# Three 256-column products per k-tile in the MLP up-projections, summed in half a PSUM bank

## The chip, the cores and the metric

The kernel runs on one core of a Trainium2 chip, in one launch. The metric is the device time of one execution in microseconds (us); shorter is better. The profile is of one execution, recorded on the same core, and its times are microseconds from the first instruction unless they are marked ns. PE is TensorE's stream of matrix products and PEld its stream of weight loads, DVE is VectorE, ACT is ScalarE, POOL is GpSimd and SP is SyncE.

## The reference, cut to what matters

The model is a trunk of two layers on 256 tokens of width 2048. Layer 0 has a bidirectional state-space mixer with a gated output, layer 1 has windowed attention. After each of the two stands the same kind of MLP, and only its first half is touched here:

```python
def rms_norm(x, gain):
    y = xf * lax.rsqrt(jnp.mean(xf * xf, axis=-1, keepdims=True) + NORM_EPS)
    return y * gain

def sqrelu_mlp(h, w_up, w_down):          # w_up 2048 x 8192, w_down 8192 x 2048
    return jnp.square(jax.nn.relu(h @ w_up)) @ w_down

h = h + sqrelu_mlp(rms_norm(h, mlp_norm[i]), mlp_w_up[i], mlp_w_down[i])
```

All inputs and the output are float32.

## The kernel before, in words

Products of float32 operands are made from a high and a low part. A weight block arrives by DMA (`wload`, L655 to L669), ACT rounds it to the high part `hi` (L667), and DVE subtracts to get the low part `lo` (L668). Activations are split in the same way when they are written (`norm_post`, L716, for the MLP's input). A product `x @ w` is then the sum of three: high by high, low by high, and high by low. `wnext` (L679) hands out the next split block and keeps one more in preparation; there are two buffers for raw blocks, three for high parts and three for low parts, used in turn.

`mlp` (L813) has two parts. The **up-projection** walks over 64 blocks of 128 hidden units (`fb`). For each block it takes one weight block of 16 k-tiles (128 x 128 each) and one PSUM bank of 512 float32 columns. The tokens are the moving operand. The activations lie in `act`, as 16 k-tiles, each with its high part (256 tokens) next to its low part (256 tokens). `up_mm` (L825) issues two products for each k-tile: L827 multiplies the high weights with both parts at once, 512 columns wide, so that the left half of the bank collects high by high and the right half high weights by low activations; L828 multiplies the low weights with the high activations, 256 columns wide, into the left half. So a bank ends with two halves that have to be added.

`up_post` (L830) does that: ACT copies the right half to SBUF (L832), DVE adds the left half to the copy (L834), DVE applies the rectifier and the tokens' norm factor `rb` (L835), and ACT squares into `hT` (L836). The order of issue is: products of block `fb`, then `up_post` of block `fb - 1`. The first two blocks are special: their first 12 k-tiles are issued before the last part of the layer's input is normalised (`fin`, the steps of the stage ahead), and their last 4 after it.

The **down-projection** (`down`, L874) has 64 k-tiles of 128 hidden units; for each it issues 24 products of 512 columns (L878), from the three combinations, four column blocks and two token halves, into eight banks.

Every product is issued with its own load of the stationary operand. Each engine works its queue in order. The MLP runs twice, after the state-space layer and after the attention layer.

Of the kernel before, what the change touches and what calls it, by code (L numbers as in the profile page):

```python
# [9 lines left out]
F32 = mybir.dt.float32  # L10
# [3 lines left out]
ALU = mybir.AluOpType  # L14
AX = mybir.AxisListType

P = 128
D = 2048
L = 256
# [73 lines left out]
class Ring:  # L93
# [3 lines left out]
    def next(self):  # L97
        self.i = (self.i + 1) % len(self.tiles)
        return self.tiles[self.i]
# [63 lines left out]
def drain(g):  # L163
    for _ in g:
        pass


class Kernel:
# [644 lines left out]
    def mlp(self, nxt, fin):  # L813
        nc, ar = self.nc, self.ar
        pe = nc.tensor
        last = nxt is None
        pool = Scope(ar, "ml", 2, 48128)
        rb = pool.tile([P, L], F32, name="rb", bufs=1)
        hTs = [ar.get("hT#%d" % i, [n, L], at=o) for i, (n, o) in enumerate(((32, 31744), (16, 39936), (16, 44032)))]

        def hT(kt):
            return hTs[0][:, kt] if kt < 32 else hTs[kt // 16 - 1][:, kt % 16]
        act = self.act

        def up_mm(bk, wh, wl, kts):  # L825
            for kt in kts:
                pe.matmul(bk, lhsT=wh[:, kt], rhs=act[:, kt].rearrange("p x c -> p (x c)"), start=(kt == 0), stop=False)  # L827
                pe.matmul(bk[:, :L], lhsT=wl[:, kt], rhs=act[:, kt, 0], start=False, stop=(kt == KT - 1))  # L828

        def up_post(fb, bk):  # L830
            t = pool.tile([P, L], F32, name="up_t")
            nc.scalar.copy(t, bk[:, L:])  # L832
            s = pool.tile([P, L], F32, name="up_s")
            nc.vector.tensor_add(s, bk[:, :L], t)  # L834
            nc.vector.scalar_tensor_tensor(s, s, 0.0, rb, op0=ALU.max, op1=ALU.mult)  # L835
            nc.scalar.activation(hT(fb), s, AF.Square)  # L836

        def wup():
            return (w.rearrange("p (k c) -> p k c", k=KT) for w in self.wnext())
        early = []  # L840
        next(fin)
        next(fin)
        for fb in range(2):
            wh, wl = wup()
            bk = self.bank()
            up_mm(bk, wh, wl, range(12))
            early.append((bk, wh, wl))
            next(fin)
        drain(fin)
        for tt in range(2):  # L850
            self.norm_end(tt)
        for fb in range(2):
            up_mm(*early[fb], range(12, KT))
        self.rstd_row(rb)
        for fb in range(2):
            up_post(fb, early[fb][0])
        post = None
        for fb in range(2, FF // P):
            wh, wl = wup()
            bk = self.bank()  # L860
            up_mm(bk, wh, wl, range(KT))
            if post:
                up_post(*post)
            post = (fb, bk)
        NK = FF // P

        def split(kt):
            hh = pool.tile([P, L], F32R, name="hh", bufs=3)
            hl = pool.tile([P, L], F32R, name="hl", bufs=3)
            nc.scalar.copy(hh, hT(kt))  # L870
            nc.vector.tensor_sub(hl, hT(kt), hh.bitcast(F32))  # L871
            return hh, hl

        def down(kt, tt, hh, hl, wh, wl, cbs=range(4)):  # L874
            ts = slice(tt * P, (tt + 1) * P)
            for x, w in ((hh, wh), (hl, wh), (hh, wl)):
                for cb in cbs:
                    pe.matmul(bks[tt][cb], lhsT=x[:, ts], rhs=w[:, cb * 512:(cb + 1) * 512],  # L878
                              start=(kt == 0 and w is wh and x is hh), stop=(kt == NK - 1 and w is wl))
        nx = split(0)  # L880
        w0 = self.wnext()
        up_post(*post)
        ar.free("act")
        bks = [[self.bank() for _ in range(4)] for _ in range(2)]
        pend = []
        for kt in range(NK):
            hh, hl = nx
            wh, wl = self.wnext() if kt else w0
            if kt + 1 < NK:
                nx = split(kt + 1)  # L890
            if kt == NK // 2 + 4 and not last:
                ar.free("hT#0")
                hx = ar.get("hx", [2, 4, 512], at=31744)
                gains = ar.get("hg", [D], at=35840)
                nc.sync.dma_start(gains, self.d["gains"][nxt])
            if kt < NK - 2:
                for tt in range(2):
                    down(kt, tt, hh, hl, wh, wl)
            else:
                pend.append((kt, hh, hl, wh, wl))  # L900
        ar.free("hT")
        if not last:
            self.norm_begin(nxt)

        def end(tt, cb):
            cs = slice(cb * 512, (cb + 1) * 512)
            gain = None if last else gains[:, cs]
            nc.vector.tensor_add(self.resid[:, tt, cs], self.resid[:, tt, cs], bks[tt][cb])
            if last:
                nc.sync.dma_start(self.d["out"][:, tt, cs], self.resid[:, tt, cs])  # L910
            else:
                self.norm_pre(cb, tt, gain, hx[:, tt, cb])
                if cb == 3:
                    self.norm_end(tt)

        def post(tt):
            for cb in range(4):
                self.norm_post(cb, tt, hx[:, tt, cb])
                yield
        for tt in range(2):  # L920
            n = 0 if last else len(pend) - 1
            for p in pend[:n]:
                down(p[0], tt, *p[1:])
            for cb in range(4):
                for p in pend[n:]:
                    down(p[0], tt, *p[1:], cbs=(cb,))
                end(tt, cb)
        pool.close()
        if not last:
            drain(post(0))  # L930
            return post(1)
# [466 lines left out]
```

## Time and profile before

| what | value |
|---|---|
| time, median of 3 runs | 2107.94 us (2106.41 to 2108.83) |
| profiled execution, first to last instruction | 2103.6 us |
| PE busy | 2030.6 us, 13,844 products |
| PEld busy | 1705.0 us, 13,844 loads |
| DVE busy | 1245.0 us |
| ACT busy | 974.7 us |
| up-projection of the first MLP | 386 to 757 us |
| up-projection of the second MLP | 1394 to 1751 us |

The profiled execution has no device time of its own beside its span; the three timed runs lie 2.8 to 5.2 us above that span, for what happens ahead of the first and behind the last instruction. In a table of stretches, each engine's busy time in the stretch is followed by the number of instructions in brackets, and PEclk is the clock granted to TensorE as a share of full speed. In a list of groups, the columns are line, engine, operation, output and inputs, shapes and count, then busy time and the mean of one in ns, then the idle time just before them and what ended it. A product's own duration contains the time it takes to run through the array, which overlaps with the product behind it; the time that one costs in a dense stream is the distance from its start to the next start.

### The profile page before, as it was taken

The page shows a single profiled execution, that of the slowest core. Times are in us where ns is not written, and L with a number is a line of the kernel's source. Part 1 is how long each engine was busy: PE and PEld are TensorE (multiplying, and loading weights), DVE is VectorE, ACT ScalarE, POOL GpSimd, SP SyncE. Part 2 cuts the span into 40 slices and gives each one's busy share as a digit, 9 for nine tenths or more (in the row PEclk, how much of TensorE's full clock was granted, in tenths as well). Part 3 has the DMA queues.
Part 4 walks back from the last instruction along what each step waited for, and adds up shares of the span by engine and source line. Part 5 has one row for each costly group of instructions (what it writes and reads, how often), then busy time and mean ns, then how long its engine had stood idle before and what let it go on. Part 6 is the DMA issues. An engine that isn't in the chain of part 4 may idle for free.

```text
span 2103.6 us, 33054 instructions
## 1 busy us (share of the span) xinstructions
PE 2030.6 (97%) x13844; PEld 1705.0 (81%) x13844; DVE 1245.0 (59%) x1824; ACT 974.7 (46%) x1238; POOL 331.0 (16%) x248
## 2 busy tenths in 40 slices
PE   4989999999999999999999889999999999999999
PEld 4877778788888888888887667888888888888887
DVE  8889736655555554444556877465555555444444
ACT  6553645444444444434434556554444444443442
POOL 6988721200000000000003330100000000000000
PEclk9999999999999999999999999999999999999999
DMA  3224455455555555655554332455555555555554
GB/s 120 73 93 144 152 199 196 154 200 188 193 180 184 193 184 200 213 188 199 202 186 153 115 128 96 146 185 200 188 193 186 195 184 196 200 187 193 200 187 153
DMA packets 59685, 364.28 MB, mean 173 GB/s; under 512 B 6816, under 2 KB 9152, under 8 KB 19600
## 3 DMA queue, kind: packets, MB, share of 16 engines
q1 hardware_dynamic: 54144, 342.32, 46.4%
q10 hardware_dynamic: 5184, 19.49, 2.8%
q8 instruction: 108, 1.77, 0.3%
q0 software_dynamic: 208, 0.36, 0.0%
q14 instruction: 41, 0.34, 0.0%
HBM read 360.05 MB, written 2.10 MB: 172 GB/s over the span
## 4 chain that ended last, share of the span: by engine, by line
PE 75%; DVE 4%; ACT 2%; DMA 1%; issue 1%; POOL 0%; SPq 0%; ACTq 0%; DVEq 0%
PE bank L878 33%; PE bank L827 23%; PE bank L828 11%; PE bank L686 2%; PE bank L687 2%; PE bank L688 2%; DVE slot L668 1%; ACT slot L667 1%; ACT slot L1039 1%; PE bank L1058 1%; DMA slot<-in_wqkv 1%; PE bank L1049 1%; DVE slot L1043 1%; DVE slot L1024 1%; DMA slot<-in_wup 0%
## 5 line engine op out<-in xcount | busy, mean ns | idle before, releaser
L668 DVE TENSOR_TENSOR slot<-slot,slot 128x2048 fp32r<-128x2048 f32 (+1 forms) x321 | 713.6, 2225 | 737.0 <-ACT slot L667 733.3
L667 ACT CAST slot<-slot 128x2048 fp32r<-128x2048 f32 (+2 forms) x357 | 623.5, 1752 | 743.0 <-PE bank L878 368.4
L827 PE MATMUL bank<-slot,slot 128*128 128x512 f32 x2048 | 720.0, 397 | 0.0
L878 PE MATMUL bank<-slot,slot 128*128 128x512 f32 x3072 | 696.7, 389 | 0.0
L878 PEld LDWEIGHTS bank<-slot,slot 128*128 128x128 f32 x3072 | 576.5, 188 | 119.6
L828 PE MATMUL bank<-slot,slot 128*128 128x256 f32 x2048 | 572.0, 280 | 0.0
L827 PEld LDWEIGHTS bank<-slot,slot 128*128 128x128 f32 x2048 | 385.5, 188 | 92.5
L828 PEld LDWEIGHTS bank<-slot,slot 128*128 128x128 f32 x2048 | 386.9, 189 | 0.3
L686 PE MATMUL bank<-slot,slot 128*128 128x512 f32 x544 | 217.3, 401 | 6.8 <-ACT slot L667 5.2
L688 PE MATMUL bank<-slot,slot 128*128 128x512 f32 x544 | 207.7, 395 | 8.3 <-POOL slot L668 8.1
L687 PE MATMUL bank<-slot,slot 128*128 128x512 f32 x544 | 213.6, 393 | 0.0
L686 PEld LDWEIGHTS bank<-slot,slot 128*128 128x128 f32 x544 | 102.7, 189 | 31.4 <-ACT slot L667 6.5
L836 ACT ACTIVATE slot<-slot 128x256 f32<-128x256 f32 x128 | 53.6, 420 | 160.4 <-DVE slot L835 160.4
L688 PEld LDWEIGHTS bank<-slot,slot 128*128 128x128 f32 x544 | 101.6, 188 | 32.0 <-POOL slot L668 10.1
L687 PEld LDWEIGHTS bank<-slot,slot 128*128 128x128 f32 x544 | 102.8, 189 | 20.4 <-issue 0.5
L668 POOL TENSOR_TENSOR slot<-slot,slot 128x1024 fp32r<-128x1024 f32 (+2 forms) x36 | 101.1, 2818 | 102.5 <-ACT slot L667 97.2
L949 POOL DMA_DIRECT2D slot<-in_pos x1 | 0.8, 754 | 613.1 <-DVE slot L871 613.1
L532 DVE TENSOR_TENSOR bank<-bank,slot 128x256 f32<-128x256 f32 x126 | 54.4, 431 | 4.1
L835 DVE SCALAR_TENSOR_TENSOR slot<-slot 128x256 f32<-128x256 f32 x128 | 54.2, 425 | 4.2
L704 POOL TENSOR_TENSOR slot<-slot 128x512 f32<-128x512 f32 x16 | 28.9, 1814 | 170.6 <-DVE slot L1157 61.5
L870 ACT CAST slot<-slot 128x256 fp32r<-128x256 f32 x128 | 51.0, 400 | 8.3 <-PE bank L878 8.3
L871 DVE TENSOR_TENSOR slot<-slot,slot 128x256 fp32r<-128x256 f32 x128 | 53.3, 419 | 1.7 <-ACT slot L870 1.6
(217 smaller groups left out, 1389.0 us busy)
## 6 DMA issues: line engine op xcount, KB each, us to landing
slot<-in_wup SPq DMA_DIRECT2D x128, 1024.0 KB, 4.8
slot<-in_wdn SPq DMA_DIRECT2D x128, 1024.0 KB, 4.8
slot<-in_wqkv SPq DMA_DIRECT2D x20, 1024.0 KB, 4.9
slot<-in_wge ACTq DMA_DIRECT2D x32, 512.0 KB, 3.7
slot<-in_wgl SPq DMA_DIRECT2D x16, 1024.0 KB, 5.3
slot<-in_wo SPq DMA_DIRECT2D x16, 1024.0 KB, 4.9
slot<-in_bz SPq DMA_DIRECT2D x16, 336.0 KB, 3.5
slot<-in_cp SPq DMA_DIRECT2D x16, 256.0 KB, 2.7
```

Of the source, the lines that this page charges most:

```text
L532: yield v.tensor_mul(xy, lb, st[:, k - 1].rearrange("p r (o g) -> p r o g", o=1).broadcast_to([P, 2, 2, n]))
L667: self.nc.scalar.copy(hi[:, c], raw[:, c])
L668: (self.nc.gpsimd if e == "g" else self.nc.vector).tensor_sub(lo[:, c], raw[:, c], hi[:, c].bitcast(F32))
L686: pe.matmul(out, lhsT=xh, rhs=wh, start=first, stop=False)
L687: pe.matmul(out, lhsT=xl, rhs=wh, start=False, stop=False)
L688: pe.matmul(out, lhsT=xh, rhs=wl, start=False, stop=last)
L827: pe.matmul(bk, lhsT=wh[:, kt], rhs=act[:, kt].rearrange("p x c -> p (x c)"), start=(kt == 0), stop=False)
L828: pe.matmul(bk[:, :L], lhsT=wl[:, kt], rhs=act[:, kt, 0], start=False, stop=(kt == KT - 1))
L835: nc.vector.scalar_tensor_tensor(s, s, 0.0, rb, op0=ALU.max, op1=ALU.mult)
L836: nc.scalar.activation(hT(fb), s, AF.Square)
L871: nc.vector.tensor_sub(hl, hT(kt), hh.bitcast(F32))
L878: pe.matmul(bks[tt][cb], lhsT=x[:, ts], rhs=w[:, cb * 512:(cb + 1) * 512], start=(kt == 0 and w is wh and x is hh), stop=(kt == NK - 1 and ...
```

## The change

`up_mm` issues three products of 256 columns for each k-tile instead of one of 512 and one of 256: high weights by high activations, high weights by low activations, and low weights by high activations. All three add into the left half of the bank, and the right half stays unused. Within a block all 32 products with high weights come first and then the 16 with low weights; before, the two kinds alternated. In `up_post` the copy and the add are gone, and the rectifier reads the left half of the bank directly. The same `up_mm` and `up_post` serve both MLPs and their first two, divided blocks.

```diff
         def up_mm(bk, wh, wl, kts):
             for kt in kts:
-                pe.matmul(bk, lhsT=wh[:, kt], rhs=act[:, kt].rearrange("p x c -> p (x c)"), start=(kt == 0), stop=False)
+                for x in range(2):
+                    pe.matmul(bk[:, :L], lhsT=wh[:, kt], rhs=act[:, kt, x], start=(kt == 0 and x == 0), stop=False)
+            for kt in kts:
                 pe.matmul(bk[:, :L], lhsT=wl[:, kt], rhs=act[:, kt, 0], start=False, stop=(kt == KT - 1))
 
         def up_post(fb, bk):
-            t = pool.tile([P, L], F32, name="up_t")
-            nc.scalar.copy(t, bk[:, L:])
             s = pool.tile([P, L], F32, name="up_s")
-            nc.vector.tensor_add(s, bk[:, :L], t)
-            nc.vector.scalar_tensor_tensor(s, s, 0.0, rb, op0=ALU.max, op1=ALU.mult)
+            nc.vector.scalar_tensor_tensor(s, bk[:, :L], 0.0, rb, op0=ALU.max, op1=ALU.mult)
             nc.scalar.activation(hT(fb), s, AF.Square)
```

## The prediction

> **What bounds the kernel now.** I read the page's head first, then its chain of waits, then tables by stretch for the two stages that the change touches.
>
> ```profile
> span 2103.6 us, 33054 instructions
> PE 2030.6 (97%) x13844; PEld 1705.0 (81%) x13844; DVE 1245.0 (59%) x1824; ACT 974.7 (46%) x1238; POOL 331.0 (16%) x248
> ...
> PE 75%; DVE 4%; ACT 2%; DMA 1%; issue 1%; POOL 0%; SPq 0%; ACTq 0%; DVEq 0%
> PE bank L878 33%; PE bank L827 23%; PE bank L828 11%; PE bank L686 2%; PE bank L687 2%; PE bank L688 2%; DVE slot L668 1%; ACT slot L667 1%; ACT slot L1039 1%; PE bank L1058 1%; DMA slot<-in_wqkv 1%; PE bank L1049 1%; DVE slot L1043 1%; DVE slot L1024 1%; DMA slot<-in_wup 0%
> ```
>
> PE carries the chain. The up-projections' two lines hold 34% of it; no line of `up_post` appears. An average over the span doesn't say that the stage itself is bound by PE, so next come the two up-projections whole, from the first L827 to the first L878:
>
> ```profile
> 386.00:756.60 370.60, 366.17 (x2063) 0.99 0.52 182
> 1394.20:1751.30 357.10, 357.10 (x2064) 1.00 0.54 189
> ```
>
> The second column is PE's busy time. In the second MLP PE never stops; in the first it stands idle for 4.43 us, in one piece ahead of a transpose:
>
> ```profile
> 390.32 0.28 PE L828 MATMUL bank<-slot,slot 128*128 128x256 f32 x1
> 395.04 0.47 PE L713 MATMUL bank<-ident,slot 128*128 128x128 f32 x1 [4.43 <-POOL slot L704]
> ```
>
> That wait is for the input's norm (L704, the gain multiply of the stage ahead), which the change leaves alone. So in both stages the time is what PE's products cost, start to start. Here is that cost, in dense stretches of the first up-projection, the first down-projection, the second up- and the second down-projection (columns: stretch, PE busy with its products, clock, DMA):
>
> ```profile
> 440.00:740.00 300.00, 300.00 (x1700) 1.00 0.53 187
> 760.00:1090.00 330.00, 330.00 (x1458) 1.00 0.56 198
> 1420.00:1740.00 320.00, 320.00 (x1847) 1.00 0.55 191
> 1760.00:2080.00 320.00, 320.00 (x1414) 1.00 0.55 194
> ```
>
> Down-projections hold only 512-column products: 330/1458 = 226.3 ns each, and 320/1414 = 226.3 in the second layer. An up-projection's k-tile is two products: 300/850 = 352.9 ns in the first layer, 320/923.5 = 346.5 in the second, for 768 columns. All four at clock 1.00.
>
> How much of that is columns? One short stretch ran at half clock; below its row in the table of stretches are two rows of the timeline:
>
> ```profile
> 396.60:400.40 3.80, 3.80 (x13) 0.50 0.00 0
> ```
>
> ```profile
> 396.59 0.63 PE L827 MATMUL bank<-slot,slot 128*128 128x512 f32 x1
> ...
> 400.43 0.63 PE L827 MATMUL bank<-slot,slot 128*128 128x512 f32 x1
> ```
>
> Between these two starts lie six k-tiles (two products each): 3.84 us, 640 ns a k-tile, 0.833 ns a column. At full clock a column is therefore 0.417 ns: 512 take 213.3, 256 take 106.7, 768 take 320.0. What is left over at full clock is 226.3 - 213.3 = 13.0 ns for a 512-column product by itself, and for the pair 26.5 ns in the second layer (13.2 a product) and 32.9 in the first (16.5 a product). In the second layer each product, wide or narrow, costs its columns and some 13 ns more.
>
> **The change part by part.** *Products.* The columns of a k-tile stay 768, but three products carry them instead of two. Nothing hides a third product's fixed cost, because PE has no gap in the stage. The trace has no stream of 256-column products only, so I bound its cost by the rows above.
>
> Second layer, 1024 k-tiles: 3 x (106.7 + 13.2) = 359.7 against 346.5, so +13.2 ns, 13.5 us in all. First layer, 1024 k-tiles less 20: 12 are issued ahead of the 4.43 us wait, which swallows their excess of 0.2 us at most, and about 8 run at half clock, where the rows show no fixed cost. The lower price for the rest is the same 359.7, +6.8 ns each, 6.8 us in 1004 tiles; with the first layer's own 16.5 a product it is 3 x 123.2 = 369.6, +16.7 ns, 16.8 us. Which? The layer's excess over the second sits in the alternating stream alone: the uniform 512-column streams cost 226.3 in both layers. The new stream is uniform in width, so I take a value nearer the lower one, +10 ns, 10.0 us. Sum: 23.5 us.
>
> *Loads.* Each product loads its stationary operand, also where it repeats: L878 uses one operand for four products in a row and has as many loads as products.
>
> ```profile
> L878 PE MATMUL bank<-slot,slot 128*128 128x512 f32 x3072 | 696.7, 389 | 0.0
> L878 PEld LDWEIGHTS bank<-slot,slot 128*128 128x128 f32 x3072 | 576.5, 188 | 119.6
> ```
>
> Can the loads keep up? Here are transposes, each with a full load, from the timeline, and their group:
>
> ```profile
> 1111.33 1.04 PE L713 MATMUL bank<-ident,slot 128*128 128x128 f32 x8
> ```
>
> ```profile
> L713 PE MATMUL bank<-ident,slot 128*128 128x128 f32 x96 | 13.9, 279 | 4.4 <-POOL slot L704 4.4
> ```
>
> So the two neighbours on one `wh` save no load, and loads rise from two to three per k-tile. Eight transposes span 1.04 us; without the last one's 0.28 that is 0.76 for seven steps, 109 ns for a load and its product. That is under the 119.9 ns that I give a 256-column product, so the loads stay hidden, with some 11 ns to spare. That cover is thin: it is a rival below.
>
> *`up_post`.* It loses one ACT copy and one DVE add for each of 128 blocks. These are the rows in the first layer's dense stretch:
>
> ```profile
> L668 DVE TENSOR_TENSOR slot<-slot,slot 128x2048 fp32r<-128x2048 f32 x53 | 121.5, 2292 | 135.0 <-ACT slot L667 135.0
> L667 ACT CAST slot<-slot 128x2048 fp32r<-128x2048 f32 x54 | 103.1, 1910 | 97.6 <-PE bank L827 94.2 <-DMA slot<-in_wup 3.4
> L835 DVE SCALAR_TENSOR_TENSOR slot<-slot 128x256 f32<-128x256 f32 x54 | 23.0, 425 | 1.8
> L834 DVE TENSOR_TENSOR slot<-bank,slot 128x256 f32<-128x256 f32 x53 | 22.1, 417 | 0.0
> L832 ACT COPY slot<-bank 128x256 f32<-128x256 f32 x53 | 19.4, 365 | 0.0
> ```
>
> That is 128 x 0.417 = 53 us less on DVE and 128 x 0.365 = 47 us less on ACT, and I give it no time: PE is busy 300.00 of 300.00 us there, DVE waits 135 us for ACT, and ACT waits 94 us for PE to give back a buffer of high weights. The remaining rectifier reads a bank instead of SBUF; the two rows of 417 (with a bank) and 425 ns (without) say that this costs between -8 and +8 ns, beside idle time. Its wait is now for the block's last product itself, which was issued a whole block (5.6 us) earlier; behind it on DVE is the split L668, whose low weights PE needs only in the next block. A bank is free one instruction sooner; no product waits for a bank today, so that is nothing too.
>
> *Order.* High weights are done with after 32 of 48 products, so ACT's cast may start a third of a block, 1.9 us, sooner, and low weights are wanted later. Both add slack where there is slack. In the first two blocks PE reaches the last of the 12 early k-tiles sooner, with their low products still queued behind; if a tile of `act` came late there, up to 12 x 0.12 = 1.4 us of work that used to fill the wait would come behind it. The one wait there begins after all 24 products of the early part, so I take 0 and keep 1.4 us for the range. No DMA is added or moved.
>
> Sum against the profiled 2103.6 us: 2127.1 us of span; the runs' median stands 4.3 us above that span, so 2131.4 us.
>
> **The rivals.**
>
> *No change, since a narrow product is cheaper than its share.* I charged the pair's fixed cost to both products evenly. The chain of waits, cut to the two dense stretches (first layer, then second), splits it otherwise:
>
> ```profile
> by line: PE bank L827 66.4%; PE bank L828 33.6%
> ```
>
> ```profile
> by line: PE bank L827 66.8%; PE bank L828 33.2%
> ```
>
> By it a narrow product holds PE for 0.336 x 352.9 = 118.6 ns or 0.332 x 346.5 = 115.0 ns. If that is its price whatever follows, three cost 355.7 (+2.8) and 345.1 (-1.4): +1.4 us, 2109. With 115.0 in both layers the first gains 7.8 ns a tile, and the time is 2098.7. It decides if the cost beyond 115 ns belongs to the wide product. Against it: a wide product among its like holds PE for 226.3 ns, and in the pair, by the same split, for 234.3 and 231.5, so some of what the split gives to the wide one comes from its narrow neighbour.
>
> *The cost goes mainly by column.* The Trainium skill, page "TensorE: Matmul & The Clock Gate", section "Back-to-back issue gap", states a gap of columns over 2.4 GHz and only 2.5 ns more a product; by that the third product would add 2.5 ns a k-tile, an estimate of 5 us in all, 2113. The 226.3 ns of this trace, with 13.0 over its columns, does not agree with it. In this kernel the mechanism would be a slower stream, 226.3/512 = 0.442 ns a column: 339.5 for 768, which leaves 3.5 ns a product in the second layer and 6.7 in the first. A third product then adds 3.6 + 6.7 = 10.3 us: 2118. Against it: the half-clock rows show 0.833 a column, exactly twice 0.417.
>
> *The narrow product bears all of the first layer's excess.* Then one costs 352.9 - 226.3 = 126.6 there and three cost 379.8: +27.0 us in 1004 tiles, with the second layer's 13.5 some 40 us: 2148. The equal 226.3 in both layers speaks for it; that the excess could as well be one of alternation, against.
>
> *Loads bound.* If a load needed 188 ns, its full duration, before the next could start, three would cost 564 ns, +430 us. The transposes' 109 ns a step speak strongly against it.
>
> **How the numbers follow.** A measurement of this kernel can tell about 0.2%, 4.2 us, from no change. Forecast (fixed cost per product, +20 to +30 us, 2128 to 2138): 0.56. By column, 2118: 0.12. All on the narrow one, 2148: 0.08. Loads: 0.02. No change or a gain: 0.22, of which 0.14 within 0.2% and 0.08 faster. Slower is the sum of the first four, 0.78. The range leaves out the loads, the top case and the gain below 2104, 0.18 in all, and reaches above the forecast's 2138 by the 1.4 us of the order and some of the way to the top case: 2104 to 2143.
>
> **What would show it.** In the changed profile, a dense stretch of each up-projection should give 16 x 3 products a block at 119 to 123 ns each, PE still without a gap, the up-projections longer by about 10 and 13 us, the down-projections unchanged, and PEld's count up by 2048. DVE's busy time should fall by 53 us and ACT's by 47 with no product starting sooner. It is wrong if narrow products run at 115 to 117 ns (first rival), if PE shows gaps ahead of products (`act`, banks or low weights late), or if a start follows its load by more than now.

## The result, and the profile after

The changed kernel takes 2127.98 us (median of 4 runs, 2126.87 to 2129.07) against 2107.19 us (4 runs, 2106.41 to 2108.83): a ratio of 1.0098, with a 95% interval from 1.0086 to 1.0110. It is slower by 20.8 us. First the head of the page after the change and its chain of waits:

```profile
span 2126.3 us, 36901 instructions
PE 2051.3 (96%) x15892; PEld 1818.2 (86%) x15892; DVE 1191.2 (56%) x1696; ACT 945.7 (44%) x1110; POOL 330.0 (16%) x248
...
PE bank L877 32%; PE bank L828 23%; PE bank L830 11%; PE bank L686 3%; PE bank L688 3%; PE bank L687 3%; POOL slot L550 2%; DVE slot L668 2%; POOL slot L491 1%; POOL slot L551 1%; ACT slot L667 1%; PE bank L636 1%; DVE slot L1042 1%; PE bank L572 1%; ACT slot L1038 1%
```

Lines have moved: L828 is now the product with high weights, L830 the one with low weights, L877 the down-projection. PE has 2048 products and as many loads more, DVE and ACT have less work, and the time is longer. The two up-projections whole, from the first L828 to the first L877 (stretch, then busy time and count of PE, PEld, DVE, ACT and POOL, then clock and DMA):

```profile
387.80:764.90 377.10, 372.20 (x3086) 371.52 (x3086) 178.50 (x166) 155.15 (x145) 8.11 (x6) 1.00 0.51 181
1402.70:1773.90 371.20, 370.36 (x3088) 370.15 (x3087) 174.38 (x158) 153.57 (x139) 2.56 (x2) 1.00 0.52 183
```

They last 377.1 and 371.2 us where they lasted 370.6 and 357.1: 6.5 and 14.1 us more, 20.6 of the 22.7 us between the two spans. (The first row of before begins 0.2 us ahead of its first product; from first product to first product the stages grew by 6.7 and 14.2 us.) PE's busy time in these rows grew by 6.0 and 13.3 us, and its idle time by 0.5 and 0.8 us: 4.43 and 0 before, 4.90 and 0.84 now. Of the 2.1 us that are left, 1.6 lie ahead of the first up-projection (it starts at 387.8 instead of 386.2), in a part that the change leaves alone; three profiles of the kernel before start it at 386.2, 385.7 and 389.1.

The spans differ by more than the medians, 22.7 against 20.8 us. Each run's time lies 1.7 to 1.8 us above its own span, so of the 4.3 us by which the median of before stood above the profiled span, some 2.5 us are a difference between executions and not, as said ahead of the prediction, what happens outside the first and the last instruction.

Another thing is new here: the loads, PEld, were busy for 318 and 312 us in these stages by the same table of the kernel before and are now busy as long as PE itself. That alone doesn't put the loads at their limit. The record of one load lasts 192 ns here, so loads that start 120 ns apart always overlap in the record. Inside, from the tables of dense stretches and from the timeline:

```profile
440.00:740.00 300.00, 300.00 (x2502) 1.00 0.52 183
760.00:1090.00 330.00, 330.00 (x1477) 1.00 0.55 196
1420.00:1740.00 320.00, 320.00 (x2669) 1.00 0.53 187
1780.00:2080.00 300.00, 300.00 (x1325) 1.00 0.54 193
```

```profile
442.30 4.00 PE L828 MATMUL bank<-slot,slot 128*128 128x256 f32 x32
446.14 2.08 PE L830 MATMUL bank<-slot,slot 128*128 128x256 f32 x16
448.06 4.00 PE L828 MATMUL bank<-slot,slot 128*128 128x256 f32 x32
```

A narrow product holds PE for 300/2502 = 119.9 ns in the first layer and 320/2669 = 119.9 in the second. (The second row begins shortly before the first up-projection ends, so it is not read; the fourth gives 300/1325 = 226.4 for a wide product, as before.) From the timeline: 48 products in 448.06 - 442.30 = 5.76 us, 120.0 each, 360.0 for a k-tile. Before, a k-tile took 352.9 and 346.5 ns.

What the lighter `up_post` did, by the groups of the first dense stretch:

```profile
L668 DVE TENSOR_TENSOR slot<-slot,slot 128x2048 fp32r<-128x2048 f32 x52 | 118.6, 2281 | 0.0
...
L667 ACT CAST slot<-slot 128x2048 fp32r<-128x2048 f32 x52 | 98.8, 1900 | 156.5 <-PE bank L828 156.5
L834 DVE SCALAR_TENSOR_TENSOR slot<-bank,slot 128x256 f32<-128x256 f32 x52 | 22.1, 425 | 163.1 <-PE bank L830 163.1
```

The rectifier (now L834) takes 425 ns from a bank, as it did from SBUF. The idle time has changed its place: before, DVE waited 135 us for ACT ahead of its splits (L668); now it waits 163 us ahead of the rectifier, for the block's own last product. Nobody on PE waits for either.

### The profile page after: what moved, and what is told of

It reads as the page before. It is cut to its first block, busy times and chain, and to the rows that moved or that the text cites. A ratio compares the mean times of both kernels' runs of the same rounds, so it can differ in the third digit from the quotient of the medians.

```text
span 2126.3 us, 36901 instructions
## 1 busy us (share of the span) xinstructions
PE 2051.3 (96%) x15892; PEld 1818.2 (86%) x15892; DVE 1191.2 (56%) x1696; ACT 945.7 (44%) x1110; POOL 330.0 (16%) x248
## 4 chain that ended last, share of the span: by engine, by line
PE 81%; DVE 6%; POOL 5%; DMA 3%; ACT 3%; issue 1%; SPq 0%; ACTq 0%; POOLq 0%; DVEq 0%
PE bank L877 32%; PE bank L828 23%; PE bank L830 11%; PE bank L686 3%; PE bank L688 3%; PE bank L687 3%; POOL slot L550 2%; DVE slot L668 2%; POOL slot L491 1%; POOL slot L551 1%; ACT slot L667 1%; PE bank L636 1%; DVE slot L1042 1%; PE bank L572 1%; ACT slot L1038 1%
## 5 line engine op out<-in xcount | busy, mean ns | idle before, releaser
L668 DVE TENSOR_TENSOR slot<-slot,slot 128x2048 fp32r<-128x2048 f32 (+1 forms) x321 | 713.9, 2227 | 441.4 <-ACT slot L667 439.3
L877 PE MATMUL bank<-slot,slot 128*128 128x512 f32 x3072 | 696.7, 389 | 0.0
L877 PEld LDWEIGHTS bank<-slot,slot 128*128 128x128 f32 x3072 | 576.6, 188 | 119.4
L828 PE MATMUL bank<-slot,slot 128*128 128x256 f32 x4096 | 515.5, 284 | 1.7 <-DVE ms L724 0.8
L828 PEld LDWEIGHTS bank<-slot,slot 128*128 128x128 f32 x4096 | 502.3, 192 | 2.5 <-DVE ms L724 1.0
L830 PE MATMUL bank<-slot,slot 128*128 128x256 f32 x2048 | 267.3, 283 | 0.0
L834 DVE SCALAR_TENSOR_TENSOR slot<-bank,slot 128x256 f32<-128x256 f32 x128 | 54.2, 425 | 379.8 <-PE bank L830 379.7
L830 PEld LDWEIGHTS bank<-slot,slot 128*128 128x128 f32 x2048 | 255.3, 192 | 0.0
L686 PE MATMUL bank<-slot,slot 128*128 128x512 f32 x544 | 217.0, 400 | 7.0 <-ACT slot L667 5.4
L688 PE MATMUL bank<-slot,slot 128*128 128x512 f32 x544 | 208.1, 395 | 7.6 <-POOL slot L668 7.5
L687 PE MATMUL bank<-slot,slot 128*128 128x512 f32 x544 | 213.8, 393 | 0.0
L668 POOL TENSOR_TENSOR slot<-slot,slot 128x1024 fp32r<-128x1024 f32 (+2 forms) x36 | 101.0, 2815 | 102.3 <-ACT slot L667 89.0
L870 DVE TENSOR_TENSOR slot<-slot,slot 128x256 fp32r<-128x256 f32 x128 | 53.3, 418 | 0.8 <-ACT slot L869 0.8
```

The costliest lines, as they stand in the source:

```text
L668: (self.nc.gpsimd if e == "g" else self.nc.vector).tensor_sub(lo[:, c], raw[:, c], hi[:, c].bitcast(F32))
L686: pe.matmul(out, lhsT=xh, rhs=wh, start=first, stop=False)
L687: pe.matmul(out, lhsT=xl, rhs=wh, start=False, stop=False)
L688: pe.matmul(out, lhsT=xh, rhs=wl, start=False, stop=last)
L828: pe.matmul(bk[:, :L], lhsT=wh[:, kt], rhs=act[:, kt, x], start=(kt == 0 and x == 0), stop=False)
L834: nc.vector.scalar_tensor_tensor(s, bk[:, :L], 0.0, rb, op0=ALU.max, op1=ALU.mult)
```

## The experiments

The theory: a float32 product costs its columns (0.417 ns each) and about 13.3 ns more, so a third product for the same columns costs 13.3 ns; and the first layer's dearer k-tile comes from alternating widths. The rivals: another part of the change matters (the order, `up_post`), or the loads, not the products, set the 120 ns.

### The order alone, twice

```diff
             for kt in kts:
                 pe.matmul(bk, lhsT=wh[:, kt], rhs=act[:, kt].rearrange("p x c -> p (x c)"), start=(kt == 0), stop=False)
+            for kt in kts:
                 pe.matmul(bk[:, :L], lhsT=wl[:, kt], rhs=act[:, kt, 0], start=False, stop=(kt == KT - 1))
```

> The kernel before with the order of the products alone changed: within a block all 16 products of 512 columns first, then all 16 of 256; the copy and the add stay. Theory (each product costs its columns and a fixed 13.3 ns, and what the first layer paid beyond that, 353.2 against 346.7 ns a k-tile, comes from alternating widths): 226.7 + 120.0 = 346.7 ns a k-tile in both layers, so about 6.6 us less than before in the first layer, nothing in the second: near 2100.6 us. Rival 1 (the first layer's excess belongs to that layer or to 512-column products into one bank, not to the alternation): 353 ns stays, 2107 us. Rival 2 (in a stream of their own, 512-column products on one bank cost more than in the down-projection): over 346.7 in both layers, slower than 2107 us.

> The order alone again (16 wide, then 16 narrow products in a block), for a second interval. Theory (no turns between widths but two in a block, so no slower pace): 347.7 to 347.9 ns a k-tile in both layers as in its first profile, times in one heap, 0.1 to 0.2% under the kernel before. Rival: no difference from the kernel before, ratio 1.000.

Measured: 2105.39 us against 2108.18, ratio 0.9986 (0.9971 to 1.0000); the second time 2105.05 against 2106.32, ratio 0.9991 (0.9980 to 1.0002). The timeline of the first, where L827 are the wide products and L829 the narrow ones:

```profile
601.36 3.82 PE L827 MATMUL bank<-slot,slot 128*128 128x512 f32 x16
605.01 2.08 PE L829 MATMUL bank<-slot,slot 128*128 128x256 f32 x16
606.93 3.82 PE L827 MATMUL bank<-slot,slot 128*128 128x512 f32 x16
...
612.50 3.82 PE L827 MATMUL bank<-slot,slot 128*128 128x512 f32 x16
```

Two blocks in 11.14 us: 348 ns a k-tile, in the first layer, where the alternating products take 353. The second profile agrees, with 1728 products in 300 us, 347.2 ns a k-tile. So the first layer's excess does go with the alternation. Its gain is small in the time, and this table and timeline of the first run say why:

```profile
386.40:751.70 365.30, 359.96 (x2062) 1.00 0.53 186
1390.70:1750.80 360.10, 358.19 (x2064) 1.00 0.55 189
```

```profile
1394.98 0.60 PE L713 MATMUL bank<-ident,slot 128*128 128x128 f32 x4
1397.48 1.20 PE L827 MATMUL bank<-slot,slot 128*128 128x512 f32 x4 [1.91 <-DVE ms L724]
```

The first up-projection is 5.3 us shorter than before (365.3 against 370.6), the second 3.0 us longer (360.1 against 357.1): its groups save nothing over the 346.5 ns there, PE's busy time is 1.1 us longer, and a wait of 1.91 us has appeared in the two divided first blocks. The first layer has such a wait too, 1.40 us ahead of an L827 at 403.13 us, while its old one is 0.5 us shorter (3.94). PE now runs sooner through the wide products whose part of `act` is there, and the narrow ones that used to fill the time until the next part comes are queued behind the ones that wait. (PE's order in these blocks isn't the program's line by line: the kernel is built with a scheduler that moves instructions, and only eight wide products of each block, not twelve, stand ahead of this wait.) Net 2.3 us, 0.1%: both intervals have it inside, and both touch or hold 1.000, so that the time is shorter isn't shown by the timed runs. That the first stage is shorter is shown by its own length: from first product to first product it takes 365.2 us in both profiles of this kernel and 370.0 to 370.3 in three profiles of the kernel before.

### Narrow products without the new order

```diff
             for kt in kts:
                 for x in range(2):
                     pe.matmul(bk[:, :L], lhsT=wh[:, kt], rhs=act[:, kt, x], start=(kt == 0 and x == 0), stop=False)
-            for kt in kts:
                 pe.matmul(bk[:, :L], lhsT=wl[:, kt], rhs=act[:, kt, 0], start=False, stop=(kt == KT - 1))
```

> The kernel after with the order undone: for each k-tile two 256-column products with high weights, then one with low weights. Theory (equal widths make a uniform stream, whatever the operands): 120.0 ns a product in both layers, the time after, 2128 us. Rival (the order of the operands is what removed the first layer's excess): some 6.5 ns a k-tile more in the first layer, 2134 us or above.

Measured: 2124.04 us (2122.38 to 2128.94), ratio 1.0065 (1.0047 to 1.0084) to the kernel before of that set.

```profile
440.00:740.00 300.00, 300.00 (x2503) 1.00 0.52 183
...
1420.00:1740.00 320.00, 320.00 (x2669) 1.00 0.53 185
```

The same 119.9 ns in both layers, so the order of the operands is of no matter to a stream of equal widths. Most of the slowdown is thus there without the new order: 15.9 us against the 20.8 of the whole change. The trace of this run has no new wait in the divided first blocks. Its up-projections take 375.6 and 370.0 us from first product to first product, and those of the whole change 377.0 and 371.1, so the new order costs 2.5 us in these stages. The rest of the difference between 15.9 and 20.8, which come from two sets of runs, isn't found there.

### The shorter post alone

```diff
         def up_post(fb, bk):
-            t = pool.tile([P, L], F32, name="up_t")
-            nc.scalar.copy(t, bk[:, L:])
             s = pool.tile([P, L], F32, name="up_s")
-            nc.vector.tensor_add(s, bk[:, :L], t)
-            nc.vector.scalar_tensor_tensor(s, s, 0.0, rb, op0=ALU.max, op1=ALU.mult)
+            nc.vector.scalar_tensor_tensor(s, bk[:, :L], 0.0, rb, op0=ALU.max, op1=ALU.mult)
```

> The kernel before with the shorter post alone: products of 512 and 256 columns as before, and the rectifier reads the left half of the bank; the copy and the add are gone, so the product of high weights and low activations, which lies in the right half, is left out of the result. Theory (ACT and DVE have slack, PE none): no change, 2107 us, k-tiles of 353 and 347 ns in the two layers as before. Rival (the 100 us of ACT and DVE work were worth something to the products, by fewer reads of PSUM or earlier buffers): below 2103 us, with shorter k-tiles.

Measured: 2107.93 us against 2108.18, ratio 0.9998 (0.9984 to 1.0012).

```profile
440.00:740.00 300.00, 300.00 (x1699) 1.00 0.54 187
...
1420.00:1740.00 320.00, 320.00 (x1847) 1.00 0.55 191
```

300/1699 and 320/1847 against 300/1700 and 320/1847 before: the products keep their pace in both layers. The copy and the add cost nothing that the pace or the timed runs show; the interval of the runs is some 3 us either way.

### What a product costs: other widths and other loads

The next runs change the shape of the up-projections' products, with half loads also the rectifier behind them. The diffs are cut to the line with high weights, or to the new lines. First six products of 128 columns for a k-tile; the product with low weights is cut in two in the same way:

```diff
-                    pe.matmul(bk[:, :L], lhsT=wh[:, kt], rhs=act[:, kt, x], start=(kt == 0 and x == 0), stop=False)
+                    for c in (slice(0, P), slice(P, L)):
+                        pe.matmul(bk[:, c], lhsT=wh[:, kt], rhs=act[:, kt, x, c], start=(kt == 0 and x == 0 and c.start == 0), stop=False, skip_group_check=True)
```

> The kernel after with every 256-column product cut in two of 128 columns: six products for a k-tile, the same 768 columns, twice the loads. Theory (13.3 ns fixed for each product, and loads hidden): 53.3 + 13.3 = 66.7 ns a product, 400 ns a k-tile against 360, some 82 us more than after, 2210 us. Rival (a load and its product can't follow the last pair in less than the 109 ns of the transposes, so the 120 ns of a 256-column product stand close to a floor of the loads): 109 ns or more a product, 654 a k-tile, some 600 us more than after, 2730 us.

Measured: 2755.7 us (2755.16 and 2756.26).

```profile
440.00:740.00 300.00, 300.00 (x2689) 1.00 0.29 99
1760.00:2060.00 300.00, 300.00 (x2689) 1.00 0.28 99
```

300/2689 = 111.6 ns a product. The theory's 66.7 falls for this width: in this stream a full load and its product follow the last pair after 111.6 ns in the mean, close to the transposes' 109. (That it is the load shows below, with half loads.) The Trainium skill, page "TensorE: Matmul & The Clock Gate", section "LDWEIGHTS (loading the stationary operand)", gives a load's columns over 1.2 as its nanoseconds, which is an estimate of 106.7 for 128 columns; the distance from load to load in this run agrees to within 5 ns. So the 120 ns of the changed kernel have some 8 ns of room over what the loads need.

Then two products of 384 columns, which stand in place of all three:

```diff
+                for w in (wh, wl):
+                    pe.matmul(bk[:, :384], lhsT=w[:, kt], rhs=act[:, kt].rearrange("p x c -> p (x c)")[:, :384], start=(kt == 0 and w is wh), stop=(kt == KT - 1 and w is wl))
```

> The kernel after with two products of 384 columns for a k-tile (768 columns as before), high weights and low weights by turns, each by all high activations and the low ones of the first 128 tokens. The low activations of the second 128 tokens are left out, and the third quarter of the bank isn't read. Theory (columns at 0.417 ns and 13.3 ns for each product): 160.0 + 13.3 = 173.3 ns a product and 346.7 a k-tile in both layers, some 27 us under the kernel after, 2101 us. Rival (the cost over the columns goes by column, 13.3 for 512, and a product of 256 stands at a floor of the loads): 384 x 0.4427 = 170.0 ns or less a product. Rival (switching operands or widths costs): above 173.3.

Measured: 2099.27 us in one run, beside 2109.35 for the kernel before.

```profile
440.00:740.00 300.00, 300.00 (x1732) 1.00 0.54 190
1420.00:1720.00 300.00, 300.00 (x1733) 1.00 0.55 191
```

300/1732.5 = 173.2 ns: 160.0 for the columns and 13.2. Widths of 256, 384 and 512 with full loads fit one line, columns at 0.417 ns and about 13 ns a product. The cost by column (170.0) is out. This run also sets the number of products apart from the number of columns: with 768 columns for a k-tile in both, two products take 346.3 ns and three take 359.7.

Now the loads: half of the weights' columns under the same products, at 256, at 128 and at 512 columns. The edit at 256 is

```diff
-                    pe.matmul(bk[:, :L], lhsT=wh[:, kt], rhs=act[:, kt, x], start=(kt == 0 and x == 0), stop=False)
+                    pe.matmul(bk[:64, :L], lhsT=wh[:, kt, :64], rhs=act[:, kt, x], start=(kt == 0 and x == 0), stop=False)
```

with the same cut to 64 columns for the low weights; the rectifier then works on 64 partitions, and a copy on DVE fills the other 64 with `rb`. The run at 128 columns cuts the loads of the six products above in the same way, and the run at 512 multiplies the high and then the low weights of each k-tile by all 512 columns of `act`.

> The kernel after with half of every load: three products of 256 columns for a k-tile, each with 64 instead of 128 columns of weights, so that half of the hidden units are left out (their place is filled with the norm factor). Theory (13.3 ns fixed for each product, loads hidden): 120.0 ns a product as in the kernel after, 2128 us. Rival (the 120 ns are a floor of the loads, close to the 111.7 of the 128-column products in the run before): about 107 to 112 ns a product, 17 to 27 us a layer's k-tiles less in all 2 x 1024, 2080 to 2105 us.

> The kernel with six products of 128 columns, with half of every load: 64 columns of weights, half of the hidden units left out. Theory (the 111.7 ns a product of the full loads were the loads' own floor, 106.7 + 5, and the product costs 53.3 + 13.3 when loads are shorter): 66.7 ns a product, 400 a k-tile, 2210 us. Rival (a product with its load has a floor near 110 ns whatever the load's width): 110 ns stays, 2750 us. Between: a load of 64 columns takes half, 53.3 + 5 = 58 ns, and would not show if the product takes 66.7.

> Two products of 512 columns for each k-tile (high weights, then low weights, by all activations), each with 64 of its 128 columns of weights; half of the hidden units are left out and the low by low product is added into a half that isn't read. 1024 columns a k-tile. Theory (13.3 ns come with a product of float32 form whatever its load): 226.7 ns a product, 453.3 a k-tile. Rival (half of the 13.3 ns come with the full load of 128 columns, as the 60.0 ns of 128-column products and the second layer's 113.3 ns of 256-column products with half loads suggest): 220.0 ns a product in at least one layer.

Measured: 2108.82, 2127.40 and 2331.34 us, one run each. Their tables, in this order:

```profile
440.00:740.00 300.00, 300.00 (x2502) 1.00 0.52 183
1420.00:1720.00 300.00, 300.00 (x2650) 1.00 0.56 197
```

```profile
440.00:740.00 300.00, 300.00 (x5004) 1.00 0.53 184
1420.00:1720.00 300.00, 300.00 (x5004) 1.00 0.54 187
```

```profile
440.00:740.00 300.00, 300.00 (x1306) 1.00 0.41 142
1560.00:1860.00 300.00, 300.00 (x1306) 1.00 0.41 143
```

With half loads a 256-column product takes 119.9 ns in the first layer and 113.2 in the second, one of 128 takes 60.0, one of 512 takes 229.7. The 60.0 shows that the 111.6 above were set by the load's width (the products with half loads also write half of the partitions, which these runs don't set apart). Beyond that neither the theory nor its rival holds: over their columns the three cost 13.2 or 6.5, 6.6, and 16.4 ns. Less load does not simply make a product cheaper, and the 13.3 ns are not one constant of every product.

Last the type, with the upper halves of the same words read as bfloat16:

```diff
+            def b(t):
+                return t.bitcast(mybir.dt.bfloat16)[:, 1::2]
...
-                    pe.matmul(bk[:, :L], lhsT=wh[:, kt], rhs=act[:, kt, x], start=(kt == 0 and x == 0), stop=False)
+                    pe.matmul(bk[:, :L], lhsT=b(wh[:, kt]), rhs=b(act[:, kt, x]), start=(kt == 0 and x == 0), stop=False)
```

> The kernel after with its up-projections' operands read as bfloat16: the upper half of each float32 word, every second element, the same number of columns and of loads; the lower halves are left out of the result. Question: is the fixed 13.3 ns a matter of the float32 form? Theory (it is: a stream of 4-byte words at its limit): under 115 ns a product, near 109 (the 2.5 ns over the columns that the Trainium skill's page 'TensorE: Matmul & The Clock Gate', section 'Back-to-back issue gap', states, an estimate of 106.7 + 2.5). Rival (the cost comes with every product and its load, whatever the type, or from the 4-byte step between elements): 120 ns.

Measured: 2090.76 us in one run.

```profile
440.00:740.00 300.00, 300.00 (x2649) 1.00 0.55 194
1420.00:1720.00 300.00, 300.00 (x2649) 1.00 0.55 194
```

113.3 ns a product in both layers, 6.6 over the columns: with bfloat16 in both operands half of the 13.3 ns is gone. Whether the stream or the load gives it, this run doesn't tell, and float32 products with half loads came to the same 113.2 in the second layer. The 2.5 ns over the columns that the Trainium skill states for the isolated gap (page "TensorE: Matmul & The Clock Gate", section "Back-to-back issue gap") were seen in none of these streams; the least are the 6.5 to 6.6 of this run and of the half loads at 256 and 128 columns.

### The kernel before, profiled again

> The kernel before, unchanged, for a second profile. Its timed runs in the first set of experiments fall in two heaps, around 2104.5 and 2112 us, those of the kernel after and of the order alone don't. Theory (products of two widths by turns settle anew in each up-projection into one of two paces, 346.7 or 353.3 ns a k-tile, which differ by 6.7 us over a layer): the profile shows each layer at one of these two paces from its first few blocks to its end, and the span fits: about 2097, 2103.5 or 2110 us with none, one or both layers at the slower pace. Rival (the two heaps have to do with another stage): both layers as in the first profile, 353.2 and 346.9, whatever the span.

> The same once more: a third profile of the kernel before, with the same expectations; between the three profiles at least one layer should show the other pace than in the first profile if the theory of two paces holds and the span is in the other heap.

Measured: spans of 2104.5 and 2108.1 us. The dense stretches of the one, then of the other:

```profile
440.00:740.00 300.00, 300.00 (x1699) 1.00 0.54 187
1420.00:1740.00 320.00, 320.00 (x1849) 1.00 0.55 191
```

```profile
440.00:740.00 300.00, 300.00 (x1700) 1.00 0.53 187
1420.00:1740.00 320.00, 320.00 (x1848) 1.00 0.54 190
```

Three profiles of this kernel show the same two paces, 353 in the first layer and 346 in the second. The theory that each execution settles anew falls as far as these profiles go; the pace goes with the layer. The 3.6 us between these two spans aren't in these stages: the first up-projection starts at 385.7 us in the one and at 389.1 in the other. What spreads single runs from 2103 to 2115 us stays open, and none of the slowest was profiled.

## Why the prediction was right, point by point

*PE bounds both stages, and nothing hides a third product.* Right, and shown: the post alone changes nothing that the runs can tell (0.9998, from 0.9984 to 1.0012), and 20.6 us of the longer span lie inside the two up-projections. One sign of being wrong that the prediction names did come, in small: PE has new gaps ahead of products in the divided first blocks, 1.3 us net.

*A narrow product costs 106.7 + 13.2 = 119.9 ns.* Right: 119.9 by the table, 120.0 by the timeline. That I could take it from a pair of unlike products rested on one observation: in the second layer the pair's remainder was twice that of a lone wide product. To share it evenly was a choice that the trace of before could not decide, since the chain of waits split it otherwise. The 384-column run shows the line holds between. It also bears out the 0.417 ns a column, which had been taken from the half-clock rows as if they held no fixed cost: from 256 to 384 columns a product grows by 53.3 ns, 0.416 a column.

*Second layer +13.5 us.* Measured 14.1, of which 13.3 are PE's products. The surplus has a place: a gap of 0.84 us in the divided first blocks, in the timeline after the change. The first layer has two such gaps; its rows come first:

```profile
403.85 0.50 PE L828 MATMUL bank<-slot,slot 128*128 128x256 f32 x2 [0.68 <-ACT slot L716]
404.58 1.09 PE L828 MATMUL bank<-slot,slot 128*128 128x256 f32 x7 [0.23 <-DVE slot L716]
...
1407.49 0.48 PE L828 MATMUL bank<-slot,slot 128*128 128x256 f32 x2
1408.81 1.09 PE L828 MATMUL bank<-slot,slot 128*128 128x256 f32 x7 [0.84 <-DVE ms L724]
```

This is the cost of the order, of which I took 0 and kept 1.4 us for the range: the narrow products without the new order have no such gap. I looked for it at the one wait of the first layer, which became shorter (4.00 instead of 4.43 us). It came behind that wait, at 403.85 and 404.58, and in the second layer, where PE had no wait before.

*First layer +10.0 us.* Measured 6.5, of which 6.0 are PE's products and 0.5 the waits. The lower end of that term, 6.8, was the right value. I had put 3.2 us on top because I gave the layer's excess only in part to the alternation; the order-only run shows that it goes with the alternation (348 against 353 ns), and in a uniform narrow stream nothing of it is left. This is the term that was mis-sized: 3.5 us too much here and 0.6 too little in the second layer turn 23.5 into the 20.6 us of the two stages, and put the measured 2127.98 us at the lower edge of the forecast's 2128 to 2138. That the medians differ by nearly the same, 20.8, is in part chance, since the profiled spans differ by 22.7.

*`up_post` is worth nothing.* Right, with sizes wrong beside it. DVE's busy time fell by 53.8 us (53 said), ACT's by 29.0 instead of 47. The first agreement is luck: with the post alone DVE's busy time fell by 43.2 us only (1201.8 in its page), and the rest came with the order. For ACT the timeline of the kernel before shows one reason: the copy starts before the cast ahead of it has ended, and the square before the copy has, so that taking the copy out frees less than its duration. The post alone took 40.7 us off ACT (934.0 in its page); the order gave some of it back: with the post alone the square still starts 0.1 us before the cast has ended, and in the changed kernel it comes 0.43 us after it, so that both count in full.

```profile
620.90 1.91 ACT L667 CAST slot<-slot 128x2048 fp32r<-128x2048 f32 x1 [3.48 <-PE bank L827]
622.71 0.37 ACT L832 COPY slot<-bank 128x256 f32<-128x256 f32 x1
622.97 0.42 ACT L836 ACTIVATE slot<-slot 128x256 f32<-128x256 f32 x1
```

And the rectifier's wait, which I put at none because its product "was issued a whole block (5.6 us) earlier", is now all of DVE's idle time in the dense stretch: the 163.1 us ahead of L834 above, some 3.1 us a block. That a product was issued earlier does not mean that it has run: DVE reaches the rectifier before PE has done the block's last product. The shorter post alone brings half of it, 78.9 us ahead of the rectifier and 76.6 ahead of the splits in the same stretch; with the new order, which releases the casts earlier, the wait for the casts is gone and the whole of it lies there. It costs no time, since PE has no gap in the stretch; the likely reason, not tested by itself, is that the split queued behind it serves a later block.

*Loads stay hidden, with 11 ns to spare.* Right in kind; in a stream of such products the loads need 111.6 ns and not the transposes' 109, so 8 ns are left. PEld's busy time, 371.5 of 377.1 us, says nothing about this room, for the reason given with the result.

*The rivals.* A narrow product at 115.0 to 118.6 ns, one at 126.6 ns in the first layer, a cost mainly by column, and loads at 188 ns: the table after the change rules out the first two and the last, the 384-column run the third.

What remains open is what the 13.3 ns are. For float32 products with full loads they behave as a fixed price from 256 to 512 columns. Half loads and bfloat16 move them to values between 6.5 and 16.4, and one kernel shows two values in its two layers. No run here tells whether it is the read of the operands, the load or their phase to each other.

## What to carry to other kernels

Where TensorE is the bound, count products as well as columns: here each float32 product of 256 to 512 columns with a full load, among its like, cost 13 ns over its columns, so that 512 + 256 beat three times 256 by 13 ns a k-tile in one layer and by 7 in the other, while some 80 us less of VectorE and ScalarE work bought nothing. Before cutting a product, look at how long the loads need: at 128 columns they, and not the products, set the pace. When widths must be mixed, grouping equal ones took 5 us from one stage here, but added 2 to 3 us to the other, half of it or more in waits of blocks whose input comes late; the grouping with those first blocks left as they were wasn't tried.

## What the runs showed of the hardware that was not expected

- Alternating 512- and 256-column products run at one pace in one stage and at another in the next (353 and 346 ns a pair), the same in three profiled executions, though the shapes are the same; 16 and 16 in groups run at 347 to 348 in both. Why one stage pays for the turns and the other doesn't stays open.
- Half loads did not make a product of 512 columns cheaper: 229.7 ns on one bank, against 226.4 with full loads in the down-projection (four banks in turn) and 228 in the order-only kernel's groups of 16 on one bank (3.65 us, the turn to narrow products included).
- The same kernel with half loads ran 256-column products at 119.9 ns in its first up-projection and at 113.2 in its second.
